# Layer 2 of a hybrid trunk on one Trainium2 core: split weights and mixed operands kept in device memory and reloaded, and products placed in another order

## Chip, core, metric

The kernel runs on one core of a Trainium2 chip. The core has five engines with a queue each: PE (TensorE, the matmuls), DVE (VectorE), ACT (ScalarE), POOL (GpSimd) and SP (SyncE, which here issues every DMA). Each engine works through its own queue in order; a semaphore makes one wait for another. The metric is the time of one execution in device microseconds, lower is better.

## What is computed

A trunk of four layers over 256 context and 1024 grid tokens of width 1024: layers 0 and 3 are gated linear recurrences, layer 1 an mLSTM, layer 2 an RWKV-7 mixer. The change is in layer 2 alone:

```
xs = h[None] + (shifted - h)[None] * mu[:, None, None, :]          # six mixtures of h and its shifted self
r, k, v, z = einsum('gbtd,gde->gbte', xs[:4], w_rkvz)              # four products, 1024 x 1024 each
w_pre = w0 + tanh(xs[4] @ w1) @ w2;   a = sigmoid(a0 + (xs[5] @ a1) @ a2)
s = s * w_t - (s @ kk_t) (kk_t * a_t) + v_t k_t ;  y_t = s @ r_t   # per head and direction, over all tokens
y = (groupnorm(y) + bonus) * silu(z) @ w_out
```

All in float32 to the accuracy of a split: every operand of a large product is taken as a high part (`hi`, cast to the PE's fp32r) and a low part (`lo`, the remainder), and three products hi*hi, lo*hi and hi*lo are summed.

## The kernel before

Layer 2 lies in one function, `rwkv_scan`. Tokens are five blocks of 256: block 0 is the context, 1 to 4 the grid. Two kinds of work are written into one program order:

- The scan. Heads go in pairs (`e` = 0 to 7), blocks in the order `i` = 0 to 4, from both ends for the two directions: 40 batches. A batch has four generators: `prep` (decays, scores of chunk against chunk on PSUM pool `px`, masks on DVE, copies on ACT), `inverse` (of triangular 64 x 64 matrices, PSUM pool `pi`), `chain` (four steps of state, PSUM pool `pc`) and `finish` (normalisation). Each generator yields the due time of its next piece, in a unit that counts 40 to a batch; a heap merges them by due time. So `yield z + 8` sets a place in the program order and not a time. After that the order on PE, DVE, ACT and POOL is fixed by dependencies; that of SP's DMAs is chosen by the scheduler of the language.
- The dense products. `stream` takes a list of passes. A pass multiplies one 128-column strip of a weight matrix (`rows`), or, for the value `v`, 256 tokens by 512 columns (`cols`), with eight operand tiles of a `Job`. `fill` spreads the passes over the batches: group G1 (blocks 1 and 4) in batches 0 and 1, G2 (blocks 2 and 3) in 2 to 5, all the rest in 6 to 37, the end of the output product in 38 to 40. Where a stream ends its passes are drained and the next one begins with nothing loaded. Block 0 (G0) goes ahead of the scan, with `early` set.

For every weight strip of every pass, `load` fetches `wraw`, and `split` makes `whi` on ACT (L954 in the page) and `wlo` on POOL (L88, the helper `tt`). A strip serves three groups, and its split is made for each: 276 splits in all. For every job `mixed` loads a tile of h (`hp`), scales it on ACT (`mx`, L864), adds the shifted part on DVE, and splits it on ACT (`xh`, L886) and POOL (`xl`). Products r, k and v are made in two waves of half the columns, z likewise, so that `mixed` runs twice for the same operand.

In the chain a step of two directions and two heads has, in the order of the code, the products named in the rows by line: state against scores (L1358), `U` against the inverse (L1364), the state's increment (L1372), then, after the state update on DVE (`self.stt`, a helper, L83), the two output products (L1381 and L1383):

```
yield z + 8                       # L1372: ps[.., 128:192] = BT x UV
yield z + 9.2                     # DVE: next state = state * W + ps[.., 128:192]
yield z + 11.5                    # L1381, L1383: ps[.., 192:256] = X x state + RB x UV
```

All four products of a step write one PSUM tile, `pc`.

Of the kernel before, what the change touches and what calls it, by code (L numbers as in the profile page):

```python
# [10 lines left out]
F32 = mybir.dt.float32  # L11
F32R = mybir.dt.float32r
# [18 lines left out]
class Net:  # L31
# [756 lines left out]
    def rwkv_scan(self, es, hd, zd, yd, xd):  # L788
        nc = self.nc
        gate = self.mod["gate"]  # L790
        V, G, S = nc.vector, nc.gpsimd, nc.scalar
        mm = nc.tensor.matmul
# [49 lines left out]
        def mixed(g, k, blks, xs):  # L842
# [45 lines left out]
            self.lo(V if early and k % 2 else G, lo[:, 0:n], t[:, 0:n], hi[:, 0:n])  # L888

# [21 lines left out]
        def rows(job, w_ap, done):  # L911

            n, ks = job.n, len(job.tiles)
            aps = [w_ap[:, k * 128:k * 128 + 512] for k in range(0, ks, 4)]
# [8 lines left out]
        def cols(job, i, w_ap, done):  # L923

            def steps(after):
                acc = [bank(pz, "pz") for _ in range(2)]
                for k in range(8):
                    def mms(w):
                        for c in range(2):
                            tk = slice(i * 256 + c * 128, i * 256 + c * 128 + 128)  # L930
                            mm(acc[c], job.xs[k][0][:, tk], w[0], start=k == 0, stop=False)
                            mm(acc[c], job.xs[k][0][:, tk], w[1], start=False, stop=False)
                            mm(acc[c], job.xs[k][1][:, tk], w[0], start=False, stop=k == 7)
                    yield mms
                for c in range(2):
                    done(c, acc[c])
            return job, [w_ap[:, k * 512:k * 512 + 512] for k in range(8)], 1, steps, 6

        def stream(passes):
# [3 lines left out]
            raws, ready, work = [], [], []  # L943

            def load():
                if aps:
                    raws.append(tile_("wraw", [128, 512]))
                    nc.sync.dma_start(out=raws[-1], in_=aps.pop(0))

            def split():  # L950
                raw = raws.pop(0)
                hi, lo = tile_("whi", [128, 512], F32R), tile_("wlo", [128, 512], F32R)
# [11 lines left out]
            for no, (job, _, per, steps, cost) in enumerate(passes):  # L964
# [4 lines left out]
                for k, step in enumerate(steps(work.append)):  # L969
                    if k % per == 0:  # L970
                        if k:
                            ready.pop(0)
                        if not ready:
                            g = split()
                            start(g)
                        drain(ready[0][1])
# [4 lines left out]
                    if k % per == 0:  # L981
                        if len(ready) < 2 and raws:
                            g = split()
                            start(g)
                        load()
                    if nxt is not job:
# [7 lines left out]
        def group(blks, what, wave=0):  # L994
            n = 256 * len(blks)
            for g in what:
                job = Job(blks, [lambda xs, g=g, k=k: mixed(g, k, blks, xs) for k in range(8)])
                if g >= 4:
# [5 lines left out]
                    yield rows(job, self.a["r7_l1"][g - 4], done)  # L1004
                elif g == 2:
                    for i, b in enumerate(blks):
# [6 lines left out]
                        yield cols(job, i, self.a["r7_wv"][wave], done)  # L1013
                else:
                    for e in range(4 * wave, 4 * wave + 4):
# [13 lines left out]
                        yield rows(job, self.a["r7_w"][g, e], done)  # L1029

        def output(blks, ks, src):
# [17 lines left out]
            for e in range(8):  # L1049
# [7 lines left out]
                yield rows(job, self.a["r7_w_out"][e][:, ks[0] * 128:], done)  # L1057
# [34 lines left out]
        def prep(n):  # L1092
# [8 lines left out]
            raw2 = tile_("w2r", [128, 256])  # L1101
# [44 lines left out]
            for d in (0, 1):  # L1146
# [15 lines left out]
                EN, EP = tile_("EN", [128, 4, 65]), tile_("EP", [128, 4, 65])  # L1162
# [26 lines left out]
            for d in (0, 1):  # L1189
                z = 40 + 4 * d  # L1190
# [8 lines left out]
                yield z + 2  # L1199
# [5 lines left out]
                yield z + 3.3  # L1205
# [128 lines left out]
        def chain(n):  # L1334
# [16 lines left out]
            for step in range(4):  # L1351
# [27 lines left out]

                for d, hh, r in dh:  # L1380
                    mm(ps[r, d, 192:256], b[d]["X"][:, cs[d], hh, 64:128], ZV[:, d, cs[d], hh, :], start=d == 0, stop=False)  # L1381
                for d, hh, r in dh:
                    mm(ps[r, d, 192:256], b[d]["RB"][r, cs[d], :], UV[r, d, cs[d], hh, :], start=False, stop=d == 1)  # L1383
                yield z + 13
# [90 lines left out]
        for d in (0, 1):  # L1475
# [11 lines left out]
                (stream(both(*(group(g, krv, 1) for g in (G0, G1, G2)), *(group(g, (3,), w) for g in (G0, G1, G2) for w in (0, 1)),  # L1487
# [58 lines left out]
        last = {}  # L1546
# [133 lines left out]
```

## Time and profile before

| | |
|---|---|
| runs | 4802.85, 4804.9, 4807.65 us (median 4804.9) |
| profiled execution | 4822.84 us, its span 4820.1 us |
| PE, DVE, ACT, POOL busy, share of the span | 85%, 60%, 44%, 49% |
| granted TensorE clock, mean over the span | 0.881 |
| the scan of layer 2 (first to last product of the chain) | 2105.7 to 4202 us |

The profiled execution is one of its own, 0.4% over the median. Busy times on PE are of pipelined matmuls, so a busy PE is not one at its peak. A wait is listed with the instruction that waited and the one that ended it.

### The profile page before, as it was taken

Reading aid. Unit: us, or ns where it says so; the run is one execution under the profiler, and the core shown is the slowest. Engines: PE = TensorE matmul, PEld = TensorE weight load, DVE = VectorE, ACT = ScalarE, POOL = GpSimd, SP = SyncE. Lnnn points to the kernel's source line nnn. Section 1 sums busy time; section 2 is a strip of 40 time slices with the busy share of each in tenths; the row PEclk is TensorE's granted clock in tenths of the full one; section 3 lists DMA queues with packets and bytes.
Section 4 is the critical chain, followed back from the end, with each engine's and each line's share of the span. In section 5 each row is a group of like instructions: output and inputs, shape, how many; then the busy total and the mean of one; then the engine's idle time right before and its main releaser. Section 6 shows DMA issues by size and latency. Waiting matters only on the chain. (4 is left out here: it accounts for less than half of the span.)

```text
span 4820.1 us, 114497 instructions
## 1 busy us (share of the span) xinstructions
PE 4105.9 (85%) x47428; PEld 3294.7 (68%) x47428; DVE 2911.4 (60%) x5216; ACT 2129.3 (44%) x4596; POOL 2360.5 (49%) x2188
## 2 busy tenths in 40 slices
PE   6999989999999897685878886888888888769988
PEld 3687768889999786564656665666665666557766
DVE  4478656444544624755655666675866566457885
ACT  3576332222222202555555554445555443347661
POOL 2466532333333322466655556555655555347662
PEclk9999989999999998787888887787898887879999
DMA  5311322222322424343433333332433344231123
GB/s 213 101 48 49 140 89 77 86 93 95 110 86 86 148 63 134 111 144 118 138 122 113 114 108 108 105 96 86 126 113 112 113 126 130 94 118 48 50 85 107
DMA packets 317863, 506.43 MB, mean 105 GB/s; under 512 B 55168, under 2 KB 201600, under 8 KB 317216
## 3 DMA queue, kind: packets, MB, share of 16 engines
q1 hardware_dynamic: 317344, 499.12, 31.9%
q8 instruction: 373, 6.11, 0.5%
q14 instruction: 146, 1.20, 0.1%
HBM read 406.02 MB, written 92.96 MB: 104 GB/s over the span
## 5 line engine op out<-in xcount | busy, mean ns | idle before, releaser
L88 POOL TENSOR_TENSOR wlo<-wraw,whi 128x512 fp32r<-128x512 f32 (+3 forms) x437 | 709.5, 1624 | 969.0 <-DVE whi L103 462.6
L114 PE MATMUL pm<-hhi,wlo 128*128 128x512 f32 (+1 forms) x1648 | 611.2, 373 | 33.8 <-POOL wlo L88 33.8
L113 PE MATMUL pm<-hlo,whi 128*128 128x512 f32 (+1 forms) x1648 | 619.6, 376 | 9.9 <-DVE hlo L83 9.9
L112 PE MATMUL pm<-hhi,whi 128*128 128x512 f32 (+1 forms) x1648 | 617.6, 375 | 0.6 <-ACT hhi L290 0.6
L112 PE MATMUL pz<-xh,whi 128*128 128x512 f32 (+1 forms) x784 | 384.2, 491 | 66.6 <-ACT whi L954 46.9
L114 PEld LDWEIGHTS pm<-hhi,wlo 128*128 128x128 f32 x1648 | 315.7, 192 | 88.9 <-POOL wlo L88 39.9
L103 DVE CAST whi<-wraw 128x1024 fp32r<-128x1024 f32 (+4 forms) x189 | 166.1, 879 | 328.1 <-PE pm L113 164.2
L88 POOL TENSOR_TENSOR xl<-mx,xh 128x512 fp32r<-128x512 f32 (+1 forms) x240 | 286.7, 1204 | 155.9 <-ACT xh L886 126.7
L113 PEld LDWEIGHTS pm<-hlo,whi 128*128 128x128 f32 x1648 | 315.9, 192 | 65.2 <-DVE hlo L83 11.4
L112 PEld LDWEIGHTS pm<-hhi,whi 128*128 128x128 f32 x1648 | 316.3, 192 | 53.4 <-issue 1.7
L114 PE MATMUL pz<-xh,wlo 128*128 128x512 f32 (+1 forms) x784 | 315.7, 403 | 29.4 <-POOL wlo L88 28.6
L112 PE MATMUL pm<-yhi,whi 128*128 128x512 f32 (+1 forms) x816 | 304.8, 378 | 41.6 <-DVE x L83 15.8
L113 PE MATMUL pz<-xl,whi 128*128 128x512 f32 (+1 forms) x784 | 317.5, 405 | 10.9 <-POOL xl L88 10.9
L113 PE MATMUL pm<-ylo,whi 128*128 128x512 f32 (+1 forms) x816 | 306.1, 376 | 6.0 <-POOL ylo L88 4.7
L83 DVE SCALAR_TENSOR_TENSOR mx<-hp,vecs,mx 128x256 f32<-128x256 f32 (+3 forms) x280 | 239.3, 880 | 116.5 <-ACT mx L864 115.4
L114 PE MATMUL pm<-yhi,wlo 128*128 128x512 f32 (+1 forms) x816 | 300.1, 375 | 2.5 <-POOL wlo L88 2.5
L83 DVE SCALAR_TENSOR_TENSOR x<-pm,mod,x 128x512 f32<-128x512 f32 (+1 forms) x208 | 136.6, 665 | 188.4 <-PE pm L114 173.3
L112 PEld LDWEIGHTS pz<-xh,whi 128*128 128x128 f32 x784 | 171.5, 219 | 112.4 <-ACT whi L954 67.1
L1297 DVE TENSOR_TENSOR D<-D,pi 128x256 f32<-128x256 f32 x160 | 67.3, 420 | 276.0 <-PE pi L1294 146.7
L1210 DVE TENSOR_TENSOR X<-px,mk 64x512 f32<-64x512 f32 x160 | 110.1, 688 | 188.9 <-PE px L1204 185.9
L88 POOL TENSOR_TENSOR t<-t,kin 128x256 f32<-128x256 f32 x88 | 84.3, 959 | 279.0 <-DVE t L1161 263.3
L699 POOL TENSOR_SCALAR kw<-kt,tkwgt 128x128 f32<-128x128 f32 x144 | 104.2, 727 | 233.4 <-PE pa L701 192.7
(345 smaller groups left out, 11038.4 us busy)
## 6 DMA issues: line engine op xcount, KB each, us to landing
wraw<-in_r_w SPq DMA_DIRECT2D x144, 256.0 KB, 3.1
kin<-r7krk SPq DMA_DIRECT2D x72, 384.0 KB, 3.8
mw<-in_mod_w SPq DMA_DIRECT2D x48, 512.0 KB, 8.1
mw<-in_mod_w SPq DMA_DIRECT2D x96, 256.0 KB, 2.5
wraw<-in_lru_w_in SPq DMA_DIRECT2D x40, 512.0 KB, 3.6
hp<-r7h SPq DMA_DIRECT2D x160, 128.0 KB, 2.2
wraw<-in_r_wv SPq DMA_DIRECT2D x80, 256.0 KB, 2.7
UZ<-r7v SPq DMA_DIRECT2D x160, 128.0 KB, 3.3
```

The source lines that it names most:

```text
L83: i = eng.scalar_tensor_tensor(out=out, in0=in0, scalar=scalar, in1=in1, op0=op0, op1=op1, **k)
L88: eng.tensor_tensor(out=out, in0=a, in1=b, op=op)
L103: nc.vector.tensor_copy(out=hi, in_=raw)
L112: mm(out, w[0][:, c], x[0][:, a:a + b], start=first, stop=False)
L113: mm(out, w[0][:, c], x[1][:, a:a + b], start=False, stop=False)
L114: mm(out, w[1][:, c], x[0][:, a:a + b], start=False, stop=last)
L699: G.tensor_scalar(out=kw, in0=kt[:, t], scalar1=gt["wgt"][:, c, d, h:h + 1], scalar2=None, op0=ALU.mult)
L1210: V.tensor_tensor(out=X[o, :, hh, :], in0=p3[o], in1=mk[d][o].unsqueeze(1).to_broadcast([64, 4, 128]), op=ALU.mult)
L1297: V.tensor_tensor(out=D, in0=D32, in1=ps[:, :, 32:64], op=ALU.add)
```

## The change

Weights: after its first split in layer 2 a strip's `whi` and `wlo` are written to device memory (`wsp`), 0.25 MB each; later passes with the same strip load both into a pair of tiles and do no split. Strips of the two low-rank projections (`l1`) are not kept. Operands: `xh` and `xl` of r, k and v are written to device memory in the first wave (`xsp`), and in the second wave `again` loads them; the z product takes all eight strips of columns in one go, so that its operand is mixed once. `whi` and `wlo` have three buffers and not two, and `w2r`, `EN` and `EP` one and not two.

Order: in `cols` the two products with `whi` stand ahead of the ones with `wlo`; in the chain the output products follow the increment at once and the state update comes behind them; the scores of `prep` have other due times.

```diff
             self.lo(V if early and k % 2 else G, lo[:, 0:n], t[:, 0:n], hi[:, 0:n])
+            if g < 3:
+                if k == 0:
+                    xsp[g, blks] = [self.dram(f"r7x{g}_{blks[0]}_{j}", (2, 128, n)) for j in range(8)]
+                for j, x in enumerate((hi, lo)):
+                    nc.sync.dma_start(out=xsp[g, blks][k][j], in_=x.bitcast(F32))
+
+        def again(g, k, blks, xs):
+
+            xs[k] = parts(k, 256 * len(blks))
+            for j, x in enumerate(xs[k]):
+                nc.sync.dma_start(out=x.bitcast(F32), in_=xsp[g, blks][k][j])
+            yield
...
                             mm(acc[c], job.xs[k][0][:, tk], w[0], start=k == 0, stop=False)
-                            mm(acc[c], job.xs[k][0][:, tk], w[1], start=False, stop=False)
-                            mm(acc[c], job.xs[k][1][:, tk], w[0], start=False, stop=k == 7)
+                            mm(acc[c], job.xs[k][1][:, tk], w[0], start=False, stop=False)
+                        for c in range(2):
+                            tk = slice(i * 256 + c * 128, i * 256 + c * 128 + 128)
+                            mm(acc[c], job.xs[k][0][:, tk], w[1], start=False, stop=k == 7)
...
             def load():
-                if aps:
-                    raws.append(tile_("wraw", [128, 512]))
-                    nc.sync.dma_start(out=raws[-1], in_=aps.pop(0))
+                if not aps:
+                    return
+                name, ap = aps[0]
+                if name not in wsp:
+                    if len(raws) < 2:
+                        aps.pop(0)
+                        raws.append((name, tile_("wraw", [128, 512])))
+                        nc.sync.dma_start(out=raws[-1][1], in_=ap)
+                elif len(ready) < 3 and not raws:
+                    aps.pop(0)
+                    w = pair()
+                    for j in (0, 1):
+                        nc.sync.dma_start(out=w[j].bitcast(F32), in_=wsp[name][j])
+                    ready.append((w, iter(())))
...
                 self.lo(V if early else G, lo, raw, hi)
+                if name[0] != "l1":
+                    d = self.dram("r7s" + "_".join(map(str, name)), (2, 128, 512))
+                    for j, t in enumerate((hi, lo)):
+                        nc.sync.dma_start(out=d[j], in_=t.bitcast(F32))
+                    wsp[name] = d
...
-                job = Job(blks, [lambda xs, g=g, k=k: mixed(g, k, blks, xs) for k in range(8)])
+                job = Job(blks, [lambda xs, g=g, k=k, f=again if wave else mixed: f(g, k, blks, xs) for k in range(8)])
...
-                    for e in range(4 * wave, 4 * wave + 4):
+                    for e in range(8) if g == 3 else range(4 * wave, 4 * wave + 4):
...
-                z = 40 + 4 * d
+                z = 40 + 4.5 * d
...
-                yield z + 2
+                yield z + 1.5
...
-                yield z + 3.3
+                yield z + 2.8
...
+                yield z + 8
                 if not last:
-                    yield z + 8
                     for d, hh, r in dh:
                         mm(ps[r, d, 128:192], b["BT"][:, d, cs[d], r], UV[:, d, cs[d], hh, :], start=True, stop=True)
-                    yield z + 9.2
+
+                for d, hh, r in dh:
+                    mm(ps[r, d, 192:256], b[d]["X"][:, cs[d], hh, 64:128], ZV[:, d, cs[d], hh, :], start=d == 0, stop=False)
+                for d, hh, r in dh:
+                    mm(ps[r, d, 192:256], b[d]["RB"][r, cs[d], :], UV[r, d, cs[d], hh, :], start=False, stop=d == 1)
+                yield z + 10
+                if not last:
...
```

Three places show the order. The first is PE in the chain, between two levels of an inverse; `UZ` holds U and the states, and a row's bracket names the semaphores that it waits for. Before, the output products stand behind dense products and wait for DVE (L1381):

```order
L1372 MATMUL pc<-UZ,BT 64x64 [waits Activation_49]
L1372 MATMUL pc<-UZ,BT 64x64 x3
L1284 MATMUL pi<-E,O 32x32 [waits DVE_49,PE_49]
L1284 MATMUL pi<-E,O 32x32 x31
...
L1381 MATMUL pc<-UZ,X_20461 64x64 [waits DVE_49]
L1381 MATMUL pc<-UZ,X_20461 64x64
L1381 MATMUL pc<-UZ,X_20509 64x64 x2
L1383 MATMUL pc<-UZ,RB_20462 64x64 x2
L1383 MATMUL pc<-UZ,RB_20510 64x64 x2
```

In the change, where the lines are 1409, 1412 and 1414, they follow the increment and wait for nothing:

```order
L1409 MATMUL pc<-UZ,BT 64x64 [waits Activation_49]
L1409 MATMUL pc<-UZ,BT 64x64 x3
L1412 MATMUL pc<-UZ,X_23124 64x64 x2
L1412 MATMUL pc<-UZ,X_23218 64x64 x2
L1414 MATMUL pc<-UZ,RB_23125 64x64 x2
L1414 MATMUL pc<-UZ,RB_23219 64x64 x2
L1331 MATMUL pi<-D,QQ 32x32 [waits Activation_49]
```

The increment now ends a run of three products, and the DVE's update is tied to the last of them.

The second is POOL in one and the same batch (the nineteenth), from `X0` of `prep` on. Before, it has splits of operands and weights between the scan's work:

```order
L88 TENSOR_TENSOR wlo_31828<-wraw_31598,whi_31827 128x512
L88 TENSOR_TENSOR X0_31923<-AR_31575,W0_31521 64x4x128
L1073 COPY kq_31942<-rn_31939 128x512
L88 TENSOR_TENSOR xl_31945<-mx_31881,xh_31944 128x512
L88 TENSOR_TENSOR X1_31998<-AR_31720,W1_31712 64x4x128
L88 TENSOR_TENSOR xl_31981<-mx_31902,xh_31980 128x512
L88 TENSOR_TENSOR wlo_31987<-wraw_31830,whi_31986 128x512
L1350 COPY UZ_31869<-st10_16494 64x64 x2
L1350 COPY UZ_31869<-st11_16495 64x64 x2
```

In the change the same stretch is:

```order
L88 TENSOR_TENSOR X0_31634<-AR_31290,W0_31243 64x4x128
L1110 COPY kq_31663<-rn_31660 128x512
L88 TENSOR_TENSOR X1_31698<-AR_31432,W1_31425 64x4x128
L1387 COPY UZ_31582<-st10_16590 64x64 x2
L1387 COPY UZ_31582<-st11_16591 64x64 x2
```

Four of nine rows are gone. Over the program, ACT has 92 casts of `whi` and not 276, POOL 184 fewer `wlo` and 96 fewer `xl`, ACT 96 fewer `mx` and 96 fewer `xh`, DVE 128 fewer parts of `mx`.

The third is SP in the value product of group G1. Before, one load of 256 KB for a strip:

```order
L1125 DMA kin_18694<-r7krk 128x768
L1102 DMA w2r<-in_r_l 128x256
L948 DMA wraw<-in_r_wv 128x512 x8
L1011 DMA r7v<-po 64x8x64 x4
L948 DMA wraw<-in_r_wv 128x512
L1311 DMA UZ<-r7v 64x2x256
```

In the change, two for a strip, with the scan's `UZ` between them:

```order
L1162 DMA kin_18806<-r7krk 128x768
L975 DMA wlo<-r7sv_5 128x512
L1139 DMA w2r<-in_r_l 128x256
L975 DMA whi<-r7sv_6 128x512
L975 DMA wlo<-r7sv_6 128x512
L975 DMA whi<-r7sv_7 128x512
L975 DMA wlo<-r7sv_7 128x512
L975 DMA whi<-r7sv_0 128x512
L975 DMA wlo<-r7sv_0 128x512
L975 DMA whi<-r7sv_1 128x512
L975 DMA wlo<-r7sv_1 128x512
L1348 DMA UZ<-r7v 64x2x256
```

SP issues 2594 DMAs in the change and 2106 before.

## Rows read from the trace of the kernel before

**Rows 1.** The page's first part, and the answer on cores.
```profile
PE 4105.9 (85%) x47428; PEld 3294.7 (68%) x47428; DVE 2911.4 (60%) x5216; ACT 2129.3 (44%) x4596; POOL 2360.5 (49%) x2188
core 0: 4820.1 us, clock 0.881
```

**Rows 2.** Busy time by stretch: columns in the first line.
```profile
core 0: us, PE busy (x) PEld busy (x) DVE busy (x) ACT busy (x) POOL busy (x), PEclk, DMA share, GB/s
1925.00:2100.00 175.00, 127.17 (x1092) 100.76 (x1090) 118.31 (x195) 103.31 (x233) 96.15 (x113) 0.73 0.42 131
2100.00:2551.00 451.00, 335.98 (x5609) 247.30 (x5611) 257.61 (x477) 237.71 (x577) 271.83 (x280) 0.82 0.40 123
2551.00:3330.00 779.00, 632.24 (x13032) 482.79 (x13031) 494.06 (x1011) 400.18 (x1088) 446.46 (x511) 0.80 0.34 106
3450.00:3782.00 332.00, 283.83 (x6420) 205.70 (x6416) 228.99 (x461) 186.45 (x532) 184.06 (x214) 0.90 0.34 106
2100.00:4205.00 2105.00, 1706.41 (x34365) 1287.63 (x34363) 1326.97 (x2683) 1060.34 (x2861) 1190.97 (x1332) 0.82 0.37 114
```

**Rows 3.** Waits of PE, 2100 to 4205 us: total, times, longest.
```profile
PE pz L932 <- POOL wlo L88: 53.7, 27, 5.5
PE px L1134 <- POOL w L88: 48.3, 19, 4.4
PE pz L112 <- ACT whi L954: 46.9, 5, 21.7
PE pc L1381 <- DVE UZ L83: 42.1, 29, 8.0
PE px L1204 <- ACT RB L1214: 29.5, 38, 4.9
PE pz L114 <- POOL wlo L88: 27.7, 7, 10.1
PE pi L1284 <- DVE E L1298: 24.5, 11, 7.3
...
PE pz L931 <- ACT whi L954: 13.7, 6, 5.8
```

**Rows 4.** Groups by line and form, 2100 to 4205 us: busy, mean ns, idle before.
```profile
L88 POOL TENSOR_TENSOR wlo<-wraw,whi 128x512 fp32r<-128x512 f32 x239 | 315.5, 1321 | 254.4 <-ACT whi L954 231.7 <-issue 11.1 <-PE px L1204 7.6
L88 POOL TENSOR_TENSOR xl<-mx,xh 128x512 fp32r<-128x512 f32 x148 | 200.9, 1367 | 91.9 <-ACT xh L886 71.8 <-ACT xh L1043 8.8 <-PE pz L113 3.0
L88 POOL TENSOR_TENSOR xl<-mx,xh 128x256 fp32r<-128x256 f32 x48 | 37.4, 787 | 37.5 <-ACT xh L886 30.1 <-ACT xh L1043 7.1
L954 ACT CAST whi<-wraw 128x512 fp32r<-128x512 f32 x239 | 147.1, 617 | 62.1 <-DMA wraw<-in_r_wv 28.7 <-PE pz L113 12.1 <-issue 9.6
L864 ACT ACTIVATE mx<-hp,omu 128x512 f32<-128x512 f32 x136 | 98.1, 722 | 60.3 <-POOL xl L88 51.1 <-DMA hp<-r7h 9.0
L886 ACT CAST xh<-mx 128x512 fp32r<-128x512 f32 x136 | 84.0, 618 | 79.0 <-DVE mx L83 78.0
```

**Rows 5.** Timeline of PE from 2262 us: start, us, instruction, idle before.
```profile
2264.34 0.80 PE L112 MATMUL pz<-xh,whi 128*128 128x512 f32 x1 [21.68 <-ACT whi L954]
...
2267.42 0.63 PE L113 MATMUL pz<-xl,whi 128*128 128x512 f32 x1
2267.84 0.63 PE L114 MATMUL pz<-xh,wlo 128*128 128x512 f32 x1
...
2270.78 0.40 PE L113 MATMUL pz<-xl,whi 128*128 128x512 f32 x1
2271.02 0.40 PE L114 MATMUL pz<-xh,wlo 128*128 128x512 f32 x1
...
2287.96 0.69 PE L1381 MATMUL pc<-UZ,X 128*64 128x64 f32 x8 [8.04 <-DVE UZ L83]
2288.58 0.69 PE L1383 MATMUL pc<-UZ,RB 64*64 64x64 f32 x8
2289.21 0.79 PE L112 MATMUL pz<-xh,whi 128*128 128x512 f32 x1
```

**Rows 6.** DMA issues, 2100 to 4205 us: size, median us to landing.
```profile
wraw<-in_r_w SPq DMA_DIRECT2D x122, 256.0 KB, 3.2
wraw<-in_r_wv SPq DMA_DIRECT2D x72, 256.0 KB, 2.7
```

**Rows 7.** One line's instructions on SP, 2100 to 4205 us: min/median/max ns.
```profile
L948 SPq DMA_DIRECT2D wraw<-in_r_w x122: 327/333/1491, 2099.7 to 3759.6; - x122
```

**Rows 8.** Waits of ACT for that load, 2100 to 4205 us.
```profile
ACT whi L954 <- DMA wraw<-in_r_wv: 28.7, 12, 6.9
```

**Rows 9.** One operation on DVE and on POOL, 2100 to 4205 us: min/median/max ns.
```profile
L88 DVE TENSOR_TENSOR X<-AR,W x76: 631/746/1779, 2155.9 to 4135.3; 64x512 f32<-64x512 f32 x76
L88 POOL TENSOR_TENSOR X<-AR,W x76: 1037/1102/1627, 2159.3 to 4132.4; 64x512 f32<-64x512 f32 x76
```

More of the change, by code (lines that the diff above doesn't have):

```diff
@@ L909, in make, with rows @@
                     return self.gens[-1]
-        def rows(job, w_ap, done):
+        def rows(job, name, w_ap, done, k0=0):
             n, ks = job.n, len(job.tiles)
-            aps = [w_ap[:, k * 128:k * 128 + 512] for k in range(0, ks, 4)]
+            aps = [(name + (k0 + k,), w_ap[:, k * 128:k * 128 + 512]) for k in range(0, ks, 4)]
             def steps(after):
@@ L921, in rows, with cols @@
             return job, aps, 4, steps, 3 * n / 512
-        def cols(job, i, w_ap, done):
+        def cols(job, i, name, w_ap, done):
             def steps(after):
@@ L936, in steps @@
                     done(c, acc[c])
-            return job, [w_ap[:, k * 512:k * 512 + 512] for k in range(8)], 1, steps, 6
+            return job, [(name + (k,), w_ap[:, k * 512:k * 512 + 512]) for k in range(8)], 1, steps, 6
+        wsp, xsp = {}, {}
         def stream(passes):
@@ L943, in stream @@
             raws, ready, work = [], [], []
+            pair = lambda: (tile_("whi", [128, 512], F32R, 3), tile_("wlo", [128, 512], F32R, 3))
             def load():
-                if aps:
-                    raws.append(tile_("wraw", [128, 512]))
-                    nc.sync.dma_start(out=raws[-1], in_=aps.pop(0))
+                if not aps:
[12 more added lines that the diff above has]
+                    ready.append((w, iter(())))
             def split():
-                raw = raws.pop(0)
-                hi, lo = tile_("whi", [128, 512], F32R), tile_("wlo", [128, 512], F32R)
+                name, raw = raws.pop(0)
+                hi, lo = pair()
                 ready.append(((hi, lo), g))
@@ L973, in stream @@
                         if not ready:
+                            if not raws:
+                                load()
+                        if not ready:
                             g = split()
@@ L985, in stream @@
                         load()
+                        load()
                     if nxt is not job:
@@ L1003, in done @@
                         yield
-                    yield rows(job, self.a["r7_l1"][g - 4], done)
+                    yield rows(job, ("l1", g), self.a["r7_l1"][g - 4], done)
                 elif g == 2:
@@ L1012, in done @@
                                                   in_=t[hr[j]].rearrange("p (h v) -> p h v", h=8))
-                        yield cols(job, i, self.a["r7_wv"][wave], done)
+                        yield cols(job, i, ("v", wave), self.a["r7_wv"][wave], done)
                 else:
-                    for e in range(4 * wave, 4 * wave + 4):
+                    for e in range(8) if g == 3 else range(4 * wave, 4 * wave + 4):
                         def done(ps, g=g, e=e):
@@ L1028, in done @@
                                 yield from kk_norm(e, t, n, blks)
-                        yield rows(job, self.a["r7_w"][g, e], done)
+                        yield rows(job, ("w", g, e), self.a["r7_w"][g, e], done)
         def output(blks, ks, src):
@@ L1056, in done @@
                     out_blocks(blks, lambda b: xd[e][:, b * 256:(b + 1) * 256], t)
-                yield rows(job, self.a["r7_w_out"][e][:, ks[0] * 128:], done)
+                yield rows(job, ("o", e), self.a["r7_w_out"][e][:, ks[0] * 128:], done, ks[0])
         def kk_norm(e, kt, n, blks):
@@ L1099, in prep @@
                     nc.sync.dma_start(out=raw[hr[d]], in_=ld[order[d][i]][hr[d]])
-            raw2 = tile_("w2r", [128, 256])
+            raw2 = tile_("w2r", [128, 256], bufs=1)
             nc.sync.dma_start(out=raw2, in_=self.a["r7_l2"][e])
@@ L1161, in prep @@
                 V.tensor_scalar(out=t, in0=ta, scalar1=hka[:, e:e + 1], scalar2=oka[:, e:e + 1], op0=ALU.mult, op1=ALU.add)
-                EN, EP = tile_("EN", [128, 4, 65]), tile_("EP", [128, 4, 65])
+                EN, EP = tile_("EN", [128, 4, 65], bufs=1), tile_("EP", [128, 4, 65], bufs=1)
                 S.activation(out=EN, in_=Q, func=AF.Exp, scale=DEC)
@@ L1378, in chain @@
                 yield z + 11.5
[L1380 to L1384, printed above, removed]
                 o = two(y, cs[0] * 64, (4 if i else 0) * 64 + cs[1] * 64)
@@ L1486, in rwkv_scan @@
         fill = [(stream(group(G1, (4, 5) + krv)), 0, 2, 336), (stream(group(G2, (4, 5) + krv)), 2, 6, 336),
-                (stream(both(*(group(g, krv, 1) for g in (G0, G1, G2)), *(group(g, (3,), w) for g in (G0, G1, G2) for w in (0, 1)),
+                (stream(both(*(group(g, krv, 1) for g in (G0, G1, G2)), *(group(g, (3,)) for g in (G0, G1, G2)),
                              output(G0, range(8), self.xsrc), output(G1, range(4), self.xsrc), output(G2, range(4), self.xsrc))), 6, 38, 1488),
```

## The prediction

> **What bounds the kernel now.** I read the busy times first: PE is busy for 85% of the span, no other engine for more than 60%, at a mean granted clock of 0.881 [rows 1]. The change touches layer 2 alone, so the next view is the busy time by stretch. In the scan, 2100 to 4205 us, PE is busy for 1706.4 of 2105 us, at a clock of 0.82; POOL for 1191.0, DVE for 1327.0, ACT for 1060.3 [rows 2]. So nobody is full. PE stands still for 2105 - 1706.4 = 398.6 us, and that is what the change can take from, beside the half-speed share of the clock. Third, who ends PE's waits there [rows 3]: the reader should see that no single cause stands out. The splits of weights take 53.7 + 27.7 us (the low part, POOL) and 46.9 + 13.7 us (the high part, ACT); the output products of the chain wait 42.1 us for the DVE's state update; the small low part in `prep` (POOL `w`) 48.3 us; copies of scores 29.5 us; the inverse 24.5 us. Last, the groups by form [rows 4] give the price of each operation. POOL and ACT have more idle time than work, and still PE waits for them: the engines go through an order fixed in advance, and one late instruction holds what stands behind it.
>
> **The splits that go.** 184 of the 248 splits from the scan on (276 in all, 28 of them ahead of it) become two loads. On POOL that is 184 x 1.321 = 243 us, on ACT 184 x 0.617 = 114 us [rows 4]. Of the 96 operand tiles that are no longer mixed 64 have 512 columns and 32 have 256: POOL is spared another 64 x 1.367 + 32 x 0.787 = 113 us, ACT 64 x (0.722 + 0.618) = 86 us and less per tile for the smaller ones. None of this counts by itself, since these engines idle; what counts is PE's waits. I set aside the 46.9 us of `whi` at L112: they are five waits, the longest 21.7, where a stream begins with nothing loaded, and there the first operand must still be mixed or fetched. Of the other three, 53.7 + 27.7 + 13.7 = 95.1 us, I take the share of vanished splits, 184 of 248: **-71 us**. Bounds: 0, if another wait fills each place, and -142, if everything on `whi` and `wlo` goes.
>
> **The chain's order.** L1381 no longer waits for the state update: **-42 us** [rows 3]; bounds 0 and -42. In exchange the update waits for the output products. In the timeline these take 2289.21 - 2287.96 = 1.25 us at the slow clock [rows 5], so each of 152 updates (40 batches of 4 steps, less the last step of 8) could come 1.25 us later, 190 us if PE stood still for it. I cost it at nothing: the next product on the state is due 5 units behind the update, at 2105/40 = 53 us a batch some 6.6 us, and no row of 3 us or more in PE's waits names that product and DVE. What covers it is the dense work between; it must fall below 1.25 us for the price to be due.
>
> **POOL's queue.** POOL loses 243 + 113 = 356 of 1191 us of work, 30%. The `prep` product waits 48.3 us for a small POOL operation that stands in that queue, so part of this goes. I take 40%, **-19 us**; bounds 0 and -48. The copies of scores (29.5 us) and the inverse (24.5 us) hang on ACT and DVE, which lose less; both stay, within a bound of 54 us either way. That bound also holds the new due times of the scores, the value products with `wlo` last (one product's time, 0.24 to 0.42 us, more cover for each late strip) and the single buffers of `EN`, `EP` and `w2r`: the last reader of each stands ahead of the next writer by most of a batch or by a full direction.
>
> The Trainium skill, GPSIMD Engine Reference, section 1 (Specifications), has GpSimd share its SBUF interfaces with VectorE, so that operations with two SBUF inputs slow each other. The trace agrees: the same product takes DVE 0.631 us at best and 1.779 at worst [rows 9]. By that rule DVE would gain as well; if the inverse's wait fell by the 30% that POOL loses, it would be 7 us more. My sum leaves it out.
>
> **The clock.** After the 21.68 us wait the products of 512 columns last 0.63 us and start 0.42 us apart, then 0.40 us and 0.24 us apart: PE runs at the lower of its two levels (1.2 GHz), and from 2270.78 us at the higher (2.4 GHz) [rows 5]. So a wait costs more than itself. The terms so far take 132 of 398.6 us of idle time and leave 267 of 1973 us, 13.5%. There is a stretch with about that much, 3450 to 3782 us: 48 of 332 us idle, 14.5%, at a clock of 0.90 [rows 2]. Its mix of work is lighter, so I take a third of the way from 0.82 to 0.90, 0.847: 1706.4 x (1 - 0.82/0.847) = **-54 us**. Bounds: 0 and, at 0.90, -152.
>
> **What is added.** SP issues 488 more DMAs, at 0.333 us each [rows 7] 163 us of a queue that has time; the bytes are some 120 MB more (70 written once, 46 for strips twice as large, 30 for reloaded operands, less some 25 of `hp`), so 114 GB/s over 2105 us become about 170, where the DMA engines are now busy for 37% [rows 2]. The copies to memory crowd the stage ahead of the scan most: 96 issues, 32 us, and 19 MB where 131 GB/s flow already and DMA is busy for 42% [rows 2]. There PE has 48 us of idle time as cover; without it a full 32 us. I take **+10 us**; bounds 0 and +32. A reload may start when the buffer is free, two strips ahead of its use. For a strip of `rows` that is 24 products, 5.8 us at 0.24 us each and 10 at 0.42, against two issues and 3.2 us to landing [rows 6]: covered. For a strip of the value it is 12 products, 2.9 to 5.0 us plus what the scan puts between, against 2.7 us and two issues: barely covered. Where such loads came late before, ACT waited 28.7 us in 12 times, 2.4 us each [rows 8]. I take six late ones, **+15 us**; bounds 0 and all 64 pairs, +154.
>
> **Sum.** -71 - 42 - 19 - 54 + 10 + 15 = -161 us, on an execution that took 4822.84 us with 2.7 us around its span. The median of the runs is 0.4% lower, 4804.9 us; the same share gives **4644.5 us**, 3.3% less.
>
> **Rivals.**
> - The waits move. An order fixed in advance gives PE another late producer where the split was: rows 3 have a tail of eight causes, and in 3450 to 3782 us, with hardly a wait for a split, PE is still idle for 14.5%. Then only the chain's wait and a little more goes: -45 us, 4760 us. Against it: POOL, the producer named most, has 30% less to do.
> - The clock gives more. The Trainium skill, TensorE: Matmul & The Clock Gate, section HAM oscillation, has idle gaps put PE back to its lower level each time. The timeline shows it after the 21.68 us and again after the 8.04 us wait (0.79 us for the next product) [rows 5]. If the scan reached 0.90 throughout, the term is -152: -71 - 42 - 19 - 152 + 25 = -259 us, 4547 us. Against it: the stage of 2551 to 3330 us has 0.80 with 19% idle, 2100 to 2551 us 0.82 with 26% [rows 2], so the clock does not follow idle time alone.
> - Slower: the value pairs come late. Place: the first product of a strip in the value passes, waiting for `whi` or `wlo` from memory. Price: 2.4 us for each of 64 pairs, 154 us, and no clock term: -132 + 10 + 154 = +32 us, 4837 us. It decides from (132 - 10)/64 = 1.9 us a pair on. For it: SP goes in order, and a store or a load of the scan that waits stands between the pairs. Against it: three buffers, and scan products between the dense ones.
>
> That the splits stay is excluded: the program order has 92 casts of `whi`.
>
> **How the numbers follow.** Under 0.2%, 9.6 us, nothing can be told from no change. The forecast, 4590 to 4710 us by itself, has 0.52; moved waits 0.21, of which 0.04 ends within 0.2%; the clock 0.13; late pairs 0.14, of which 0.02 within 0.2% and 0.12 slower. So faster 0.52 + 0.17 + 0.13 = 0.82, same 0.06, slower 0.12. The range leaves out nearly all of late pairs and the far half of the clock's: 4550 to 4805 us.
>
> **What would show it.** Right: PE's waits for `wlo` and `whi` under 75 us together in the scan, none of the output products on DVE, POOL busy some 350 us less, PE idle below 290 us, clock about 0.85. Wrong: waits of `pz` products on DMAs over 60 us (late pairs); idle time still near 400 us under other names (moved waits); long waits of the chain's first product on the state (the update was not covered); the stage ahead of the scan longer by over 30 us (crowded queue).

## The result, and the profile after

The change makes the kernel faster: 4600.7 us (median of four runs, 4591.8 to 4618.4) against 4806.3 us, a ratio of 0.9575, 95% interval 0.9541 to 0.961. That is 206 us less; 161 were forecast. A second series gave 4615.3 us and 0.9585 (0.9567 to 0.9603). It is the yardstick below: what a variant loses against the change is (its ratio - 0.9585) x 4810 us, since each ratio is taken on one chip. An interval of 0.002 is some 10 us, and a difference of two ratios is known to some 15 us.

The profiled execution took 4591.79 us. The page's first part:

```profile
PE 3991.3 (87%) x47428; PEld 3216.6 (70%) x47428; DVE 2753.6 (60%) x5088; ACT 1940.2 (42%) x4220; POOL 2003.8 (44%) x1908
```

Busy time by stretch, which answers to [rows 2]: after the stretch and its length come PE, PE's loads, DVE, ACT and POOL with busy us and count, then the clock, the DMA share and GB/s. The first row is the stage ahead of the scan, the second the whole scan.

```profile
1925.00:2095.00 170.00, 125.33 (x1084) 95.14 (x1083) 112.91 (x189) 99.51 (x225) 80.36 (x79) 0.76 0.83 272
2095.00:3974.00 1879.00, 1591.56 (x34350) 1215.56 (x34349) 1166.22 (x2553) 870.77 (x2483) 840.69 (x1055) 0.87 0.58 184
```

The whole gain is in the scan, 2105 to 1879 us. With the same products PE is busy for 1706.4 - 1591.6 = 115 us less, since the clock rose from 0.82 to 0.87, and idle for 287 us and not 399, 111 less. (The row of before runs 3 us further behind the scan's last products, all of them busy, so the first figure is 112 like for like.) So half of the gain is idle time and half is clock. The reader should also see POOL with 350 us less work and DVE with 161. The stage ahead, into which the copies go, has twice the transfers (272 GB/s after 131) and is no longer than before.

PE's waits, 2095 to 3974 us (total, times, longest), answer to [rows 3]; the scan's line numbers are higher by 37:

```profile
PE px L1171 <- POOL w L88: 40.5, 22, 4.0
...
PE pz L112 <- ACT whi L982: 25.4, 3, 21.8
PE pi L1321 <- DVE E L1335: 21.8, 12, 7.3
...
PE pi L1321 <- DVE E L1312: 19.9, 10, 5.2
...
PE pi L1342 <- DVE UZ L83: 8.8, 24, 1.2
PE pz L114 <- POOL wlo L88: 8.3, 6, 4.7
...
PE pz L947 <- POOL wlo L88: 3.4, 3, 1.8
PE pz L943 <- DMA whi<-r7sv: 2.6, 3, 1.3
```

Two rows of before, 2100 to 4205 us, on the same products of the inverse:

```profile
PE pi L1305 <- DVE E L1298: 2.5, 13, 0.2
...
PE pi L1284 <- DVE E L1275: 1.7, 4, 0.7
```

The splits' waits are all but gone (95.1 us to 12, and 3 us on transfers), and no output product waits for DVE. But the inverse waits more: for `E` 42 us and not 26, and for `UZ` 9 us that were not there. By its names this table bears out the prediction's first two terms. The experiments show that it misleads.

### The profile page after: what moved, and what is told of

Read it like the earlier page. It is cut to its first block, busy times and chain, and to the rows that moved or that the text cites. A ratio compares the mean times of both kernels' runs of the same rounds, so it can differ in the third digit from the quotient of the medians.

```text
span 4590.1 us, 114304 instructions
## 1 busy us (share of the span) xinstructions
PE 3991.3 (87%) x47428; PEld 3216.6 (70%) x47428; DVE 2753.6 (60%) x5088; ACT 1940.2 (42%) x4220; POOL 2003.8 (44%) x1908
## 3 DMA queue, kind: packets, MB, share of 16 engines
q1 hardware_dynamic: 387616, 629.70, 42.1%
## 5 line engine op out<-in xcount | busy, mean ns | idle before, releaser
L88 POOL TENSOR_TENSOR wlo<-wraw,whi 128x512 fp32r<-128x512 f32 (+3 forms) x253 | 467.5, 1849 | 775.3 <-DVE whi L103 458.8
L112 PE MATMUL pz<-xh,whi 128*128 128x512 f32 (+1 forms) x784 | 370.9, 474 | 54.2 <-ACT whi L982 29.7
L88 POOL TENSOR_TENSOR O<-DG,lev 128x256 f32<-128x256 f32 x200 | 149.6, 760 | 245.0 <-issue 153.0
L88 POOL TENSOR_TENSOR xl<-mx,xh 128x512 fp32r<-128x512 f32 (+1 forms) x144 | 176.3, 1233 | 148.5 <-ACT xh L886 105.2
L112 PEld LDWEIGHTS pm<-yhi,whi 128*128 128x128 f32 x816 | 156.5, 192 | 78.9 <-DVE x L83 22.1
```

Of the source, the lines that this page charges most:

```text
L88: eng.tensor_tensor(out=out, in0=a, in1=b, op=op)
L112: mm(out, w[0][:, c], x[0][:, a:a + b], start=first, stop=False)
```

## Experiments

The theory on trial was the prediction's: named waits go, each is worth its size and a share of the clock, and the work of POOL and ACT counts for nothing by itself. The rivals: waits move to another name; or what counts is the load of the helper engines. The scan runs from 5 to 8 us ahead of the first batch's chain to some 22 us behind the start of the last one's; a row of it is given for each kernel, with the columns as above.

| kernel | us | ratio to before | against the change |
|---|---|---|---|
| e1, chain's order alone | 4817.2 | 1.0013 (0.9997 to 1.0029) | (before: +6) |
| e2, all but the chain's order | 4617.7 | 0.9596 (0.9573 to 0.9618) | +5 |
| e3, operands mixed anew | 4703.1 | 0.9776 (0.9749 to 0.9803) | +92 |
| e4, weights split anew | 4681.7 | 0.9731 (0.9704 to 0.9758) | +70 |
| e6, splits' work on scratch | 4688.5 | 0.9737 (0.9717 to 0.9757) | +73 |
| e9, mixing's work on scratch | 4687.2 | 0.9739 (0.9722 to 0.9755) | +74 |
| e12, POOL's half of e6 | 4656.4 | 0.9687 (0.9664 to 0.971) | +49 |
| e13, the same as fills | 4620.2 | 0.9615 (0.9589 to 0.964) | +14 |
| e5, pairs loaded twice | 4770.0 | 0.9923 (0.9895 to 0.9952) | +163 |
| e7, change with `w` on DVE | 4537.9 | 0.943 (0.9416 to 0.9445) | -75 |
| e14, before with `w` on DVE | 4721.7 | 0.9823 (0.9797 to 0.9849) | (before: -85) |

**The chain's order, alone (e1) and taken back (e2).** The edit, in the kernel before; e2 is its reverse in the change:

```diff
+                yield z + 8
                 if not last:
-                    yield z + 8
                     for d, hh, r in dh:
                         mm(ps[r, d, 128:192], b["BT"][:, d, cs[d], r], UV[:, d, cs[d], hh, :], start=True, stop=True)
-                    yield z + 9.2
-                    for d, hh, r in dh:
...
-                        self.stt(V, o, ZV[r, d, c, hh, :], b[d]["W"][r, c:c + 1], ps[r, d, 128:192], ALU.mult, ALU.add)
-                yield z + 11.5
...
-                yield z + 13
+                yield z + 10
+                if not last:
+                    for d, hh, r in dh:
...
+                        self.stt(V, o, ZV[r, d, c, hh, :], b[d]["W"][r, c:c + 1], ps[r, d, 128:192], ALU.mult, ALU.add)
+                yield z + 11.5
```

> The kernel before with one part of the change, the chain's new order (output products ahead of the state update); splits and operands stay as before. Theory of removed waits: the 42 us of output products on DVE go and the clock gives back about 0.4 us for each us of wait, so 45 to 65 us less than before (4740 to 4760 us), no row of the output products on DVE over 3 us. Theory that waits move: PE's idle time in the scan stays within 15 us of 399 and the time within 15 us of before, since the update, 1.25 us later, holds the next product on the state or the next inverse. Theory that the splits alone carry the gain: no more than 20 us.

> The changed kernel with the chain's order as before. Theory of removed waits: additive, so the same 45 to 65 us come back (about 4645 to 4665 us if the changed kernel runs at 4600), and the wait of output products on DVE returns with some 40 us. Theory that waits move: 15 us at most. If the gain depends on both parts together (the dense work now fills less badly), more than 80 us come back.

Alone it gains nothing. The scan of e1, and its PE waits there:

```profile
2083.00:4201.00 2118.00, 1686.83 (x34333) 1279.46 (x34331) 1336.80 (x2678) 1067.10 (x2861) 1193.55 (x1330) 0.82 0.38 113
```
```profile
PE pz L932 <- POOL wlo L88: 62.3, 27, 5.6
...
PE pi L1284 <- DVE E L1298: 38.8, 21, 7.8
...
PE pi L1284 <- DVE E L1275: 15.7, 12, 4.3
...
PE pi L1324 <- ACT QP L1316: 13.8, 12, 5.0
...
PE pi L1284 <- POOL RB L88: 11.4, 7, 4.0
...
PE pi L1305 <- DVE UZ L83: 11.0, 22, 1.6
...
PE pi L1305 <- DVE E L1298: 3.8, 4, 1.7
...
PE pc L1358 <- DVE UZ L83: 1.0, 1, 1.0
```

The 42.1 us of the output products are gone, and PE is idle for 2118 - 1687 = 431 us, more than before. What took their place stands here: the inverse waits for `E` 14 + 14 us longer, for `RB` 9 and for `QP` 9, 11 under the name `UZ` where no such row stood, and the dense products for `wlo` 9. That is the rival of moved waits, for this part of the change.

The update's own reader, L1358, waits 1.0 us for it, so the state that comes later is not the reason. At L1305 the trace shows what was lost instead. That product reads `E` and no state. In the kernel before the output products stand right ahead of it on PE in all 39 places, behind L1294, from whose result DVE makes `E`; it waits 2.5 us. In e1 they stand there in none, and it waits 15 us. The name `UZ` in its row is only that of what DVE had in hand by then (DVE's rows, then PE's):

```profile
3401.56 0.45 DVE L1298 STREAM_TRANSPOSE E<-D 128x256 f32<-128x256 f32 x1
3401.93 1.18 DVE L83 SCALAR_TENSOR_TENSOR UZ<-UZ,W,pc 64x64 f32<-64x64 f32 x4
```
```profile
3402.15 0.69 PE L1305 MATMUL pi<-E,OF 32*32 32x32 f32 x32 [1.14 <-DVE UZ L83]
```

L1305 starts 0.14 us behind the end of `E`, with the four updates still under way. So the output products had covered the time in which DVE makes `E`. Whether the other rows that grew have the same reason was not shown.

In the change too the new order is worth 5 us, less than its interval: in e2 the wait of the output products returns with 25.2 us, and the inverse's for `E` falls from 42 to 25.

**One half of the change at a time (e3, e4).** In e3 the operands are mixed for each wave again, and not stored, and z runs in two waves; in e4 no split is kept:

```diff
-            if g < 3:
+            if False:
...
-                job = Job(blks, [lambda xs, g=g, k=k, f=again if wave else mixed: f(g, k, blks, xs) for k in range(8)])
+                job = Job(blks, [lambda xs, g=g, k=k, f=mixed: f(g, k, blks, xs) for k in range(8)])
...
-                    for e in range(8) if g == 3 else range(4 * wave, 4 * wave + 4):
+                    for e in range(4 * wave, 4 * wave + 4):
...
```
```diff
-                if name[0] != "l1":
+                if False:
```

> The changed kernel with the mixed operands made anew for each wave as before (POOL and ACT do that work again, and the operands are neither stored nor reloaded; z in two waves). Theory of removed waits: the splits' waits stay gone, so 70 to 90% of the gain stays: 4620 to 4665 us. Theory that it is the load of POOL and ACT that counts: POOL gets back 113 of the 356 us it was spared, so about a third of the gain in the scan (75 of 226 us) is lost: 4665 to 4690 us. Waits on whi and wlo under 30 us together by the first, and 40 or more by the second.

> The changed kernel with no weight kept: each strip is loaded raw and split for every pass, as before; operands are still made once, stored and reloaded, and the chain has its new order. Theory of removed waits: the 95 us of waits on whi and wlo return and the clock's share with them, so 120 to 180 us come back: 4720 to 4780 us. Theory of load: POOL gets back 243 of 356 us, two thirds of 226 us less what the chain gives, 100 to 130 us: 4700 to 4730 us. Theory that the splits' waits only shrank because POOL had less to do: waits on whi and wlo under 50 us together, and less than 90 us come back.

Scan of e3, then of e4:

```profile
2095.00:4068.00 1973.00, 1618.39 (x34379) 1235.75 (x34378) 1281.80 (x2683) 970.91 (x2682) 953.69 (x1151) 0.86 0.52 160
```
```profile
2084.00:4056.00 1972.00, 1629.51 (x34365) 1234.88 (x34364) 1228.26 (x2551) 966.91 (x2669) 1079.17 (x1239) 0.85 0.44 136
```

PE's waits for the splits in e4:

```profile
PE pz L947 <- POOL wlo L88: 44.3, 27, 5.1
...
PE pz L943 <- ACT whi L982: 18.0, 5, 6.1
...
PE pz L114 <- POOL wlo L88: 15.1, 8, 5.9
```

The two halves are worth about the same, 92 and 70 us. That breaks the theory of removed waits twice. In e3 the splits' waits stay gone (13 us), as that theory had it; the mixing of operands had hardly a wait of its own before (0.8 us for `xl`), and still costs no less than the splits. And in e4 PE waits for `whi` and `wlo` in the dense products 44.3 + 18.0 + 15.1 = 77 us, most of the 95 of before, while the loss stays under the 120 to 180 us expected. The theory of load came nearer for e4 (100 to 130 expected, 70 measured) and had too little for e3 (4665 to 4690); the third, for e4, had the loss right (under 90) and the waits wrong (under 50).

**The work without the waits (e6, e9).** The change as it is, and beside each reload the work that it saved, on scratch that no product reads (`lng2` is a constant tile of 512 columns). In e6 for each reloaded strip:

```diff
                     ready.append((w, iter(())))
+                    start(ghost())
+
+            def ghost():
+                t = tile_("wraw", [128, 512])
+                S.copy(out=t, in_=lng2)
+                yield
+                self.tt(G, t, lng2, t, ALU.subtract)
```

In e9, in `again`, for each of the 72 reloaded operand tiles:

```diff
             yield
+            n = 256 * len(blks)
+            t = tile_("mx", [128, 512], bufs=3)
+            S.activation(out=t[:, 0:n], in_=lng2[:, 0:n], func=AF.Identity, scale=mu[:, 0:1])
+            yield
+            self.stt(V, t[:, 0:n], lng2[:, 0:n], mu[:, 0:1], t[:, 0:n], ALU.mult, ALU.add)
+            yield
+            S.copy(out=t[:, 0:n], in_=lng2[:, 0:n])
+            yield
+            self.tt(G, t[:, 0:n], lng2[:, 0:n], t[:, 0:n], ALU.subtract)
```

> The changed kernel itself, run beside the next three on one chip as the yardstick for them: 4590 to 4615 us, within 0.3% of its first time. Against it the chain's old order (4617.7 us) stands 5 to 25 us slower.

> The changed kernel, and for each strip that is reloaded a ScalarE copy and a GpSimd subtraction of 512 columns on scratch that no product reads: the splits' work without their waits (this work is extra, and the outputs don't depend on it). Theory of removed waits: these engines have room, so 0 to 15 us more than the changed kernel. Theory of load: the small steps of the scan stand behind this work in the queues again, and 50 to 80 us come back, most of what keeping the weights gave (81 us); POOL's w, the inverse's t and RB and the copies RB then take 25 us or more of added waits of PE.

> The changed kernel, and for each of the 72 reloaded operand tiles the mixing's four operations (two on ScalarE, one each on VectorE and GpSimd) on scratch that no product reads, in the same places of the program. Theory that the operands' own waits or loads made the gain: 0 to 15 us more than the changed kernel. Theory of load: 50 to 90 us more, which is what mixing them anew cost (102 us) less the part of z's second wave.

Scans of the change in this series, of e6 and of e9:

```profile
2093.00:3996.00 1903.00, 1610.38 (x34350) 1232.81 (x34351) 1164.33 (x2553) 869.94 (x2482) 838.97 (x1054) 0.86 0.58 181
```
```profile
2100.00:4057.00 1957.00, 1635.34 (x34377) 1251.12 (x34376) 1228.13 (x2554) 965.99 (x2668) 1078.62 (x1238) 0.85 0.56 177
```
```profile
2096.00:4067.00 1971.00, 1628.60 (x34347) 1244.87 (x34348) 1239.62 (x2623) 945.86 (x2626) 929.03 (x1127) 0.85 0.56 175
```

Work that nobody waits for costs 73 us, as much as e4, where PE waits for it by name. So the splits' waits were not the main part of what the splits cost: with them or without, the same load gives the same time. One rival is left: e4 also spares the transfers of the 178 reloaded pairs, and what these cost PE under other names was not measured; by so much the waits may still count. For the operands too the work alone costs most of what mixing them anew does (74 of 92 us; e3 differs by z's second wave as well, which was not run apart). PE's wait for `w`, in the yardstick and in e6:

```profile
PE px L1171 <- POOL w L88: 35.6, 18, 3.9
```
```profile
PE px L1178 <- POOL w L88: 45.9, 24, 3.7
```

No other row grew by more: the loss is spread over many names, and half of it (25 of 54 us in the scan) is clock. One column stands out. DVE, with the same operations, is busy for 1228 us in e6 and not 1164; in e4, with the real splits, it is 1228 us too. In e9 DVE's 75 us more are another thing: 63 of them are the added mixing itself, and an operation that the others lengthen, `AR`, takes 491 ns as in the yardstick (488, below):

```profile
L88 DVE TENSOR_TENSOR AR<-kin,EN 128x256 f32<-128x256 f32 x76 | 37.3, 491 | 0.0
```

Which of the mixing's four operations costs the time, and by what way, stays open.

**Which load (e12, e13).** The next two separate two ways in which POOL's part of the splits can hurt: small steps of the scan stand behind it in POOL's queue, or its reading slows DVE. e12 keeps only POOL's operation of e6, e13 makes it fills that read nothing. Against e6:

```diff
-                S.copy(out=t, in_=lng2)
                 yield
-                self.tt(G, t, lng2, t, ALU.subtract)
+                self.tt(G, t, lng2, lng2, ALU.subtract)
```

```diff
-                S.copy(out=t, in_=lng2)
                 yield
-                self.tt(G, t, lng2, t, ALU.subtract)
+                for _ in range(3):
+                    G.memset(t[:, 0:416], 0.0)
```

> The changed kernel with only the GpSimd half of the extra work of e6_weight_ghost, a subtraction of 512 columns (1.3 us) for each reloaded strip, on scratch that no product reads, and no ScalarE copy. Theory that the load of POOL's queue is what counts: 50 to 75 us more than the changed kernel's 4615, nearly all of the 73 that both halves cost. Theory that ScalarE's queue counts as much: 20 to 45 us more.

> As e12_pool_ghost, but GpSimd fills scratch for the same 1.3 us (three fills of 416 columns) and reads nothing. Theory that small steps of the scan stand behind the work in POOL's queue: the same time as e12_pool_ghost within 15 us. Theory that GpSimd's reading slows VectorE (VectorE was busy 64 us longer with the same operations in e6_weight_ghost): VectorE's busy time in the scan falls back to about 1165 us and less than half of e12_pool_ghost's loss remains.

Groups by form in the scan (busy us, mean ns): POOL's extra work and two operations of DVE, in the yardstick, e12 and e13.

```profile
L88 DVE TENSOR_TENSOR AR<-kin,EN 128x256 f32<-128x256 f32 x76 | 37.1, 488 | 0.0
...
L1463 DVE TENSOR_TENSOR y<-y,s 128x512 f32<-128x512 f32 x15 | 10.9, 727 | 18.6 <-POOL s L1461 18.6
```
```profile
L88 DVE TENSOR_TENSOR AR<-kin,EN 128x256 f32<-128x256 f32 x76 | 53.4, 702 | 0.0
...
L1469 DVE TENSOR_TENSOR y<-y,s 128x512 f32<-128x512 f32 x15 | 19.4, 1295 | 19.4 <-POOL s L1467 19.4
...
L88 POOL TENSOR_TENSOR wraw<-lng 128x512 f32<-128x512 f32 x178 | 199.5, 1125 | 2.8
```
```profile
L88 DVE TENSOR_TENSOR AR<-kin,EN 128x256 f32<-128x256 f32 x76 | 36.8, 485 | 0.0
...
L1470 DVE TENSOR_TENSOR y<-y,s 128x512 f32<-128x512 f32 x15 | 12.0, 798 | 18.6 <-POOL s L1468 18.6
...
L983 POOL MEMSET wraw<- 128x416 f32 x534 | 237.6, 447 | 22.2
```

Their scans:

```profile
2099.00:4030.00 1931.00, 1628.97 (x34356) 1246.59 (x34355) 1222.66 (x2553) 872.96 (x2490) 1034.44 (x1233) 0.85 0.57 179
```
```profile
2095.00:4004.00 1909.00, 1610.73 (x34365) 1233.98 (x34362) 1146.68 (x2553) 872.37 (x2490) 1056.82 (x1591) 0.86 0.57 181
```

The fills hold POOL longer (237.6 us after 199.5) and cost 14 us, which is within the noise; the subtractions cost 49, and the two, run on one chip, are 36 us apart. With the subtractions `AR` takes DVE 702 ns and not 488, with the fills 485; DVE's busy time is 1223 us with the one and 1147 with the other. An operation with an input from PSUM, `D<-D,pi`, takes 420 ns in all three. So most of what POOL's subtractions cost goes with their reading and with the longer operations of DVE, and not with the time that they hold POOL's queue, though the fills made PE wait the most of all for `w`:

```profile
PE px L1178 <- POOL w L88: 54.2, 25, 5.0
```

The Trainium skill, SBUF — State Buffer, section SBUF: two separate sides, has GpSimd and VectorE share a port pair that is held for a whole instruction, and has VectorE's operations with two SBUF inputs contend only with GpSimd work that reads SBUF. By that rule the fills should leave `AR` alone, and the trace agrees, 485 ns beside 488. That the pair is held for the whole instruction no run here tests. The rest, 73 - 49 = 24 us, is what ScalarE's copies cost together with e6's slower subtraction (1339 ns and not 1125); it was not separated, and it is little more than the noise.

**The small low part `w` on VectorE (e7 in the change, e14 in the kernel before).** One letter of one line:

```diff
-self.lo(G, w2[d][hr[1 - d]], raw2[r], w2[d][r])
+self.lo(V, w2[d][hr[1 - d]], raw2[r], w2[d][r])
```

> The changed kernel with the small low part w of the prep product on VectorE instead of GpSimd. Theory of removed waits: PE's 40.5 us for w on POOL go and DVE's busy time grows little, so 15 to 40 us less than the changed kernel. Theory that waits move (as the chain's order alone did): the wait comes back under the inverse or the chain on DVE, and the time stays within 10 us.

> The kernel before, with nothing of the change but the small low part w of the prep product on VectorE instead of GpSimd. Theory that POOL's queue ahead of the scan's small steps is what counts: POOL has 356 us more work there than in the changed kernel, so w waits longer there and at least as much is gained as the 77 us in the changed kernel: 75 to 110 us less than before. Theory that this pays only once the large work has left POOL: under 40 us.

Scan and one wait of PE, of e7 and then of e14:

```profile
2095.00:3926.00 1831.00, 1570.63 (x34379) 1199.15 (x34379) 1229.86 (x2631) 871.79 (x2490) 790.74 (x983) 0.89 0.60 189
```
```profile
PE px L1171 <- DVE w L88: 1.9, 5, 1.1
```
```profile
2088.00:4101.00 2013.00, 1640.33 (x34344) 1233.27 (x34341) 1399.15 (x2754) 1061.79 (x2861) 1143.08 (x1254) 0.85 0.39 119
```
```profile
PE px L1134 <- DVE w L88: 8.1, 11, 2.0
```

A gain of 75 us in the change, far more than the 35.6 us of the wait; e7, at 4537.9 us, beats both kernels. `w` takes 0.75 us on POOL and 0.76 on DVE, so its queue changed and not its length; `AR` takes 496 ns (488 in the yardstick), so POOL's reading, of which `w` was a part, does not show in this gain. Of the 72 us that the scan loses, 32 are idle time (293 to 260) and 40 clock (0.86 to 0.89). In the kernel before the same letter gives 85 us. Here a named wait did go and was hardly replaced: 34 us of it for 32 us of idle time in the change, 40 us for 26 in the kernel before. Why this wait pays when the chain's did not, and when 19 us more of it in e13 cost next to nothing, the runs don't settle: e13 also left DVE 18 us less busy, so two effects stand against each other there.

**The reload's margin (e5).**

```diff
-                    for j in (0, 1):
+                    for j in (0, 1, 0, 1):
                         nc.sync.dma_start(out=w[j].bitcast(F32), in_=wsp[name][j])
```

> The changed kernel with each kept weight pair loaded twice, the second time onto the first (the second load is extra). Theory of hidden transfers: 0 to 10 us more, the waits on whi and wlo from memory under 15 us. Theory that loads of kept strips are at the edge (the late pairs of the prediction): each of some 160 pairs comes about 1 us later, waits of the dense products on transfers over 60 us, and 60 us or more are lost.

It lost 163 us. Waits of PE, and the longest of SP's queue, in its scan:

```profile
PE pz L943 <- DMA whi<-r7sv: 52.3, 20, 4.8
...
PE pz L112 <- DMA whi<-r7sw: 11.5, 4, 5.9
...
PE pz L947 <- DMA wlo<-r7sv: 7.0, 10, 1.4
```
```profile
SPq L975 <- DMA whi<-r7sw: 171.4, 84, 4.4
```

It does not measure traffic by itself: the second load writes the first one's tile, so SP stood still until the first had landed, and all that is behind it on SP came late too. What it shows is the mechanism of the third rival, with its price: value pairs that come late make PE wait under this name. In the change they do so for 3 to 5 us in all, so the margin was there; one more load ahead of each was too much.

## Why the prediction was right

The sign, the range and the shape were right (POOL 350 us less, idle time under 290 us, waits on `whi` and `wlo` at 40 us with the three stream starts, under the 75 named). The sum came out near the time because errors of opposite sign cancelled. Of the scan's idle time it had -132 + 15 = -117 us, measured were -111; since the terms under it were wrong one by one, that is luck, and what the sum lacked is the clock's.

- **Splits, -71 and their part of the clock.** With their share of the -54 (71 of 132) some -100; splitting anew costs 70 us, clock included. The reason was wrong in the main. The term was made from PE's waits by name; e6 brings the loss back without those waits.
- **Operands, "None of this counts by itself, since these engines idle".** This step failed. The work alone costs 74 us (e9), mixing anew 92, and the sum has for it only its part of POOL's queue below, 113 of 356 or some 6 us. An engine with idle time is not free (and in the scan POOL, busy for 1191 of 2105 us, had less of it than work): for POOL's part of the splits since its operations lengthen another engine's, for the operands in a way that the runs leave open.
- **Chain's order, -42.** Fell: 0 alone, 5 us within the change. Its wait moved to the inverse. I had costed the later update at nothing, and for its reader that holds (1.0 us at L1358 in e1). What I did not ask is what the output products covered in the place they left: at L1305 the wait rose from 2.5 us to 15.
- **POOL's queue, -19.** The wait for `w` fell by 8 us (48.3 to 40.5), 13 in the second series. Mis-sized, and the wrong question: taken off POOL altogether it is worth 75 to 85 us.
- **The clock, -54.** Mis-sized: -115 in the profiled execution, at 0.87, and -96 in the second, at 0.86, where 0.847 was taken from another stage. The rival in which the clock gives more went to 0.90; the truth lies between. One rate does not fit: against the yardstick 50 us of idle time came with 18 of busy time in e9, and against before 26 with 66 in e14.
- **The costs, +25.** Not due: late pairs 3 to 5 us after 15 forecast, the stage ahead of the scan 5 us shorter after 10 longer.
- **The rule left out.** The prediction set aside 7 us for DVE, by the Trainium skill's GPSIMD Engine Reference, section 1 (Specifications). For the splits this mattered: e12 against e13 gives 36 us to POOL's reading. For the operands it hardly did: `AR` takes 697 ns where the weights are split anew (e4) and 531 where the operands are mixed anew (e3). The row that I gave for it, `X` with 0.631 to 1.779 us, was a poor sign, since the mean of `X` hardly moves between the yardstick and e12 (918 and 957 ns). The scan of the change beside that of the kernel before shows the mechanism in operations that the change doesn't touch. The kernel before, then the change:

```profile
L88 DVE TENSOR_TENSOR AR<-kin,EN 128x256 f32<-128x256 f32 x76 | 47.2, 621 | 0.0
L83 DVE SCALAR_TENSOR_TENSOR BK<-ta,EP 128x256 f32<-128x256 f32 x76 | 47.1, 619 | 0.0
```
```profile
L88 DVE TENSOR_TENSOR AR<-kin,EN 128x256 f32<-128x256 f32 x76 | 37.7, 496 | 0.0
L83 DVE SCALAR_TENSOR_TENSOR BK<-ta,EP 128x256 f32<-128x256 f32 x76 | 36.5, 480 | 0.0
```

Taken out of the change one at a time, operands, splits and the chain's order cost 92, 70 and 5 us, 167 of some 200. The order of the value products and the due times of the scores were not run apart; nor was z in one wave.

## What to carry to other kernels

A table of waits says where time shows, not what causes it: before summing waits, ask which name takes the place of each, and settle it by adding the suspected work on scratch or by taking only the wait away. Look also at what an instruction covers in the place from which it is moved. Work on a helper engine with idle time can have a price, if it lengthens another engine's operations or stands ahead of a short one that PE needs; here a GpSimd subtraction of 1.1 us that nobody waits for cost about 0.27 us (49 us for 178), and one 0.75 us operation on the wrong queue cost 75 us for 76 of them. Where PE's clock moves with its idle time, count the clock's part from the change of busy time in a trace, not from one other stage.

## What was not expected of the hardware

Some of DVE's two-input operations are lengthened by POOL's reading, not by POOL being busy: `y<-y,s` of 512 columns took 727 ns, 1295 with the subtractions and 798 with the fills, `AR` 488, 702 and 485. Not all are: a `y<-y,s` of the same form in another line took 791, 797 and 795 ns. And the granted clock can give back more than the waits: in e7 32 us of idle time went with 40 us of busy time on the same products, at 0.86 before and 0.89 after.
